# Seven half-width products for the up projection of every second pair, and running sums copied from bank to bank by ScalarE

## The chip, the cores and the metric

The kernel runs on one core of one Trainium2 chip. The metric is the device time of one execution in microseconds (us). Weights and activations are split into a high and a low part, so that three matmuls (high by high, low by high, high by low) stand for one exact fp32 product; each full-size product therefore costs three matmuls for every 128 rows of the contraction.

## The reference

One layer of a macaron block on 512 tokens of width 1024: a SwiGLU network, a token mixer, a second SwiGLU network, each added to the stream, and a last norm. Only the two SwiGLU networks are touched here:

```python
D_MODEL = 1024
SEQ = 512
D_FF = 256 * ((8 * D_MODEL // 3 + 255) // 256)      # 2816
...
def swiglu(x, w_gate, w_up, w_down):
    return (jax.nn.silu(x @ w_gate) * (x @ w_up)) @ w_down
...
        x = x + 0.5 * swiglu(rmsnorm(x, ffn1_norm[layer]),
                             ffn1_w_gate[layer], ffn1_w_up[layer], ffn1_w_down[layer])
        x = x + token_mixer(...)
        x = x + 0.5 * swiglu(rmsnorm(x, ffn2_norm[layer]),
                             ffn2_w_gate[layer], ffn2_w_up[layer], ffn2_w_down[layer])
```

## The kernel before

Everything is kept transposed: features on the 128 partitions, the 512 tokens along the free axis. The hidden width of 2816 is 22 tiles of 128 columns, numbered j; the model width is 8 tiles, numbered k. The function `ffn` runs twice, as network "a" and network "b"; a letter a or b at the end of a tile's name tells which.

The first n1 tiles of a network (6 in a, 4 in b) are computed singly. The rest are taken two at a time by `pair(j)`: j = 6, 8, ..., 20 in a (8 pairs), j = 4, 6, ..., 20 in b (9 pairs). For a pair the gate projection is a 2-by-2 block product (two column tiles, the even and the odd k tiles, the left and the right 256 tokens), and it is done by Winograd's form of Strassen's method: seven products of half width instead of eight. Each of the seven is a call of `product`: four k tiles times three matmuls, 12 matmuls of 128x256. The sums of token blocks that it needs are made once per network (`normed_t`). The sums of weight blocks are made anew for every pair on VectorE (lines 266 to 273): `s1`, `s2`, the difference written into `r1`, and a second value of `s2`. Then each of seven weight blocks of 128x512 is split: ScalarE writes the high part (line 261), VectorE subtracts and writes the low part (line 262).

In PSUM the gate products of a pair use four banks of the tag "mm", half of each: pa (named pw), pb (px), pc (py), pd (pz). ScalarE copies the first product from pa into half of the tile `sq` (line 296), VectorE adds pb to that (298), and the further sums are made by VectorE from pd, pc and that tile (301, 302, 306, 309). The banks pa, pd and pc are used for two products each; where the second product adds into a sum that VectorE must read first, TensorE waits for that read (line 301 reads pd before the product with `a22` goes on in it; line 302 reads pc before the product with `w4`).

The up projection of a pair is done plainly by `up`, once for each of the two tiles: 8 k tiles times three matmuls of 128x512, 24 matmuls, weights loaded as one tile of 128x1024 and split by one wide cast (line 91) and one wide subtraction (line 92). VectorE then multiplies gate and up (line 313), and `activated` splits the result (lines 188 and 189) for the down projection.

What sets the order: TensorE runs in the order of the program text. ScalarE, VectorE and the DMA queue run in an order that the compiler's scheduler fixes ahead of time, from the dependences and the free buffers; on the chip each engine follows its own list strictly. The buffers matter: the tags "raw", "wh" and "wl" (incoming weights, high parts, low parts) have three buffers of 128x1024 each, "ob" (for `s1`, `s2`) two, "ptb" (for the gate tiles `g0`, `g1`) two, and PSUM has four banks "mm", two "s" and two "t". A gate product takes four wh and four wl buffers in turn, a single up tile one of each. In the first pair of each network the two up projections stand ahead of the gate products, so that there the gate products of two pairs follow one another directly.

Of the kernel before, what the change touches and what calls it, by code (L numbers as in the profile page):

```python
# [25 lines left out]
JF = FF // P  # L26
# [12 lines left out]

EARLY = (5, 3)  # L40
PAIRED = (6, 4)
HS = S // 2
F32_MAX = 3.4028234e38
PSUM = bass.MemoryType.PSUM
# [5 lines left out]
def tile_macaron(ctx: ExitStack, tc, xs, xT, wf, wgu1, wst1, wd1, wqk, wv, wo, wgu2, wst2, wd2,  # L50
                 lams, relb, onehot, addc, out):
    nc = tc.nc
    V, A, G, T = nc.vector, nc.scalar, nc.gpsimd, nc.tensor
# [13 lines left out]
    def mm_bank(nm):  # L67
        return pp.tile([P, S], F32, tag="mm", name=nm, bufs=4)
# [5 lines left out]
    sq = cp.tile([P, S], F32, tag="sq", name="sq")  # L74
# [8 lines left out]
    def load_w(src, nm, n=1024):  # L83
        raw = wp.tile([P, 1024], F32, tag="raw", name=f"raw_{nm}")
        nc.sync.dma_start(raw[:, :n], src)
        h = wp.tile([P, 1024], F32R, tag="wh", name=f"wh_{nm}")
        l = wp.tile([P, 1024], F32R, tag="wl", name=f"wl_{nm}")
        return raw, h, l

    def split_w(raw, h, l, a, b):  # L90
        A.copy(h[:, a:b], raw[:, a:b])  # L91
        V.tensor_tensor(l[:, a:b], raw[:, a:b], h[:, a:b].bitcast(F32), op=ALU.subtract)  # L92

    def get_w(src, nm, n=1024):
        raw, h, l = load_w(src, nm, n)
        split_w(raw, h, l, 0, n)
        return h, l

    def mm3(po, wh, wl, mh, ml, first, last, on=False):
        T.matmul(po, wh, mh, start=first, stop=False, skip_group_check=on)  # L100
        T.matmul(po, wh, ml, start=False, stop=False, skip_group_check=on)  # L101
        T.matmul(po, wl, mh, start=False, stop=last, skip_group_check=on)  # L102
# [72 lines left out]
    def ffn(wgu, wst, wd, n0, n1, norm, early, res, nm, hooks, first=None, last_halves=None):  # L175
# [39 lines left out]
        def t_places():  # L215
            tp.tile([P, 8], F32, tag="odd", name=f"odd{nm}", bufs=1)
            rows = [tp.tile([P, 5 * HS], F32R, tag=f"pr{p % 2}", name=f"tt{nm}{p}")
                    for p in range(4)]
            more = tp.tile([P, 12 * HS], F32R, tag="tx", name=f"tx{nm}", bufs=1)
            tl.extend(t[:, :4 * HS] for t in rows)  # L220
            th.extend(more[:, 4 * p * HS:4 * (p + 1) * HS] for p in range(3))
            th.append([t[:, 4 * HS:] for t in rows])

        def normed_t(p):
# [22 lines left out]
            c = slice(half * HS, (half + 1) * HS)  # L247
            return xh[k][:, c], xl[k][:, c]

        def pair(j):  # L250
            src = [wst[j + i - n1] for i in range(2)]
            ups = [up(j + i, src[i][1]) for i in range(2)] if j == n1 else []
            (r0, h0, l0), (r1, h1, l1) = [load_w(src[i][0], f"sg{nm}{j + i}") for i in range(2)]
            u0, u1 = slice(0, 512), slice(512, 1024)
            h2, l2, h3, l3 = [wp.tile([P, 1024], F32R, tag=t, name=f"{t}_{i}{nm}{j}")
                              for i in (2, 3) for t in ("wh", "wl")]
            s1 = tp.tile([P, S], F32, tag="ob", name=f"s1{nm}{j}")
            s2 = tp.tile([P, S], F32, tag="ob", name=f"s2{nm}{j}")

            def split(t, h, l):  # L260
                A.copy(h, t)
                V.tensor_tensor(l, t, h.bitcast(F32), op=ALU.subtract)
                return h, l

            a11 = split(r0[:, u0], h0[:, u0], l0[:, u0])
            V.tensor_tensor(s1[:], r1[:, u0], r1[:, u1], op=ALU.add)
            V.tensor_tensor(s2[:], s1[:], r0[:, u0], op=ALU.subtract)
            w2 = split(s2[:], h0[:, u1], l0[:, u1])
            w1 = split(s1[:], h1[:, u0], l1[:, u0])
            V.tensor_tensor(r1[:, u0], r0[:, u0], r1[:, u0], op=ALU.subtract)  # L270
# [6 lines left out]
            pa, pb, pc, pd = [mm_bank(f"p{c}{nm}{j}")[:, :HS] for c in "wxyz"]  # L277

            def product(po, w, mv, first, last):
                for p in range(4):  # L280
                    o = slice(p * P, (p + 1) * P)
                    mm3(po, w[0][:, o], w[1][:, o], *mv(p), first and p == 0, last and p == 3, not first)

            def b(i, half):
                return lambda p: block(2 * p + i, half)

            def t(i):
                c = slice(i * HS, (i + 1) * HS)
                return lambda p: (th[p][i] if p == 3 else th[p][:, c], tl[p][:, c])

            g0 = tp.tile([P, S], F32, tag="ptb", name=f"g0{nm}{j}")
            g1 = tp.tile([P, S], F32, tag="ptb", name=f"g1{nm}{j}")
            w = sq[:, :HS] if (j // 2) % 2 else sq[:, HS:]
            left, right = slice(0, HS), slice(HS, S)
            product(pa, a11, b(0, 0), True, True)
            A.copy(w, pa)
# [4 lines left out]
            V.tensor_tensor(g1[:, right], pd, w, op=ALU.add)  # L301
# [7 lines left out]
            V.tensor_tensor(g0[:, right], pc, w, op=ALU.add)  # L309
            A.activation(g0[:, right], g0[:, right], AF.Silu)  # L310
            for i, g in enumerate((g0, g1)):
                pu = ups[i] if ups else up(j + i, src[i][1])
                V.tensor_tensor(g[:], pu[:], g[:], op=ALU.mult)
                activated(j + i, g)

        def up(j, src):
            wh, wl = get_w(src, f"su{nm}{j}")
            pu = pp.tile([P, S], F32, tag="t", name=f"pu{nm}{j}", bufs=2)
            for k in range(KD):
                o = slice(k * P, (k + 1) * P)  # L320
# [18 lines left out]
        for j in range(j0, n1):  # L339
            mv = (eh, el) if j < n0 else (xh, xl)  # L340
            if j == 2 and first is not None:
                pg, pu = [pp.tile([P, S], F32, tag="t", name=f"p{c}{nm}2", bufs=2) for c in "gu"]
            else:
                pg = mm_bank(f"pg{nm}{j}")
                pu = mm_bank(f"pu{nm}{j}")
            for hf in range(2):
                wh, wl = get_w(wgu[j, hf], f"gu{nm}{j}_{hf}")
                for kk in range(4):
                    k = hf * 4 + kk
                    for c, pt in ((0, pg), (1, pu)):  # L350
                        o = kk * 256 + c * P
# [12 lines left out]
        for m in range(KD):  # L364
# [36 lines left out]
    with tc.manual_schedule(engines={mybir.EngineType.DVE, mybir.EngineType.Activation}):  # L401
        for t in range(4):
# [3 lines left out]
            for kk in range(2):  # L406
                k = 2 * t + kk
# [627 lines left out]
```

## Time and profile before

| | us |
|---|---|
| median of three runs | 976.99 |
| lowest and highest | 976.98 and 978.43 |
| the profiled execution | 977.07 |
| its span in the profile | 974.8 |
| TensorE busy | 961.4 (99%) |
| VectorE busy | 577.6 (59%) |
| ScalarE busy | 426.0 (44%) |

The profiled execution lies 0.08 us from the median, and 2.27 us of it lie outside the span. In the rows of the timeline the first number is the start in us from the span's start, the second the duration; then come the engine, the line, the operation and what it writes from what. PE is TensorE's matmul, DVE is VectorE, ACT is ScalarE. A matmul's recorded duration is longer than the distance to the next one, since matmuls overlap; the distance between starts is what counts.

### The profile page before, as it was taken

To read this page: it belongs to the slowest core of one execution; us is meant where nothing else is said; L and a number is where in the kernel's file an instruction comes from. 1 tells how busy PE (TensorE), PEld (TensorE's weight loads), DVE (VectorE), ACT (ScalarE), POOL (GpSimd) and SP (SyncE) were. 2 spreads that over 40 slices of the span, in tenths; PEclk is the share of its full clock that TensorE was granted. 3 is DMA by queue.
4 is the path that set the end of the run, shared out by engine and by line. 5 is a ranking of instruction groups with operands and counts; after the bars stand their busy time and mean duration, and the time that the engine had idled before them with its cause. 6 is when DMAs were issued, how large, how long until landed. Compare 5 with 4: busy or idle time off the path is not lost.

```text
span 974.8 us, 13809 instructions
## 1 busy us (share of the span) xinstructions
PE 961.4 (99%) x5394; PEld 839.6 (86%) x5394; DVE 577.6 (59%) x1108; ACT 426.0 (44%) x787; POOL 32.4 (3%) x34
## 2 busy tenths in 40 slices
PE   9999999999999999999999999999999999999996
PEld 7789998888788888988989888889988899888886
DVE  7698767765232336668764546797677566422223
ACT  6455444434232335566756554454444344322230
POOL 0000000000010110000000003000000000000110
PEclk9999999999999999999999999999999999999998
DMA  7232423224333351444342204232332233433312
GB/s 253 66 114 67 130 91 118 95 87 130 98 97 84 96 160 62 130 119 120 88 112 85 76 32 130 65 108 73 118 114 87 87 101 117 119 98 84 96 58 87
DMA packets 32720, 98.71 MB, mean 101 GB/s; under 512 B 3776, under 2 KB 6080, under 8 KB 32656
## 3 DMA queue, kind: packets, MB, share of 16 engines
q1 hardware_dynamic: 32480, 97.55, 32.8%
q8 instruction: 42, 0.69, 0.3%
q0 software_dynamic: 176, 0.30, 0.1%
q14 instruction: 22, 0.18, 0.1%
HBM read 92.55 MB, written 2.14 MB: 97 GB/s over the span
## 4 chain that ended last, share of the span: by engine, by line
PE 94%; DVE 3%; ACT 1%; DMA 1%; issue 1%; DVEq 0%; POOL 0%; ACTq 0%; POOLq 0%
PE pda L100 4%; PE pub L100 4%; PE pub L101 4%; PE pda L102 4%; PE pda L101 4%; PE pub L102 4%; PE pua L100 4%; PE pua L101 4%; PE pua L102 4%; PE pdb L101 4%; PE pdb L100 4%; PE pdb L102 4%; PE po L704 2%; PE pwo L100 1%; PE pwo L101 1%; PE pwo L102 1%
## 5 line engine op out<-in xcount | busy, mean ns | idle before, releaser
L100 PE MATMUL pda<-aha,wh_da 128*128 128x512 f32 x176 | 68.6, 390 | 0.0
L102 PE MATMUL pda<-aha,wl_da 128*128 128x512 f32 x176 | 68.5, 389 | 0.0
L101 PE MATMUL pda<-ala,wh_da 128*128 128x512 f32 x176 | 68.5, 389 | 0.0
L92 DVE TENSOR_TENSOR wl_db<-raw_db,wh_db 128x1024 fp32r<-128x1024 f32 (+1 forms) x24 | 27.3, 1136 | 62.2 <-ACT wh_db L91 62.1
L92 DVE TENSOR_TENSOR wl_da<-raw_da,wh_da 128x1024 fp32r<-128x1024 f32 (+1 forms) x24 | 27.2, 1135 | 58.7 <-ACT wh_da L91 58.6
L91 ACT CAST wh_db<-raw_db 128x1024 fp32r<-128x1024 f32 (+1 forms) x24 | 23.6, 981 | 86.2 <-PE pdb L101 78.7
L91 ACT CAST wh_da<-raw_da 128x1024 fp32r<-128x1024 f32 (+1 forms) x24 | 23.5, 981 | 84.2 <-PE pda L101 55.5
L101 PE MATMUL pdb<-alb,wh_db 128*128 128x512 f32 x154 | 59.9, 389 | 0.0
L102 PE MATMUL pdb<-ahb,wl_db 128*128 128x512 f32 x154 | 59.9, 389 | 0.0
L100 PE MATMUL pdb<-ahb,wh_db 128*128 128x512 f32 x154 | 59.9, 389 | 0.0
L100 PE MATMUL pub<-xh,wh_sub 128*128 128x512 f32 x144 | 56.1, 390 | 0.0
L101 PE MATMUL pub<-xl,wh_sub 128*128 128x512 f32 x144 | 56.1, 390 | 0.0
L102 PE MATMUL pub<-xh,wl_sub 128*128 128x512 f32 x144 | 56.0, 389 | 0.0
L670 DVE CUSTOM_DVE_ANT_0 pr<-sc,strip 128x128 f32<-128x128 f32 (+3 forms) x64 | 30.8, 488 | 34.0 <-PE sc L668 33.6
L127 POOL TENSOR_TENSOR sq<-sq,sqt 128x512 f32<-128x512 f32 x20 | 28.7, 1435 | 661.8 <-ACT sqt L126 661.8
L100 PE MATMUL pua<-xh,wh_sua 128*128 128x512 f32 x128 | 49.9, 390 | 0.0
L101 PE MATMUL pua<-xl,wh_sua 128*128 128x512 f32 x128 | 49.9, 390 | 0.0
L102 PE MATMUL pua<-xh,wl_sua 128*128 128x512 f32 x128 | 49.8, 389 | 0.0
L673 ACT ACTIVATE pr<-pr,mx 128x128 f32<-128x128 f32 (+3 forms) x64 | 36.0, 563 | 30.8 <-DVE mx L670 29.7
L100 PEld LDWEIGHTS pda<-aha,wh_da 128*128 128x128 f32 x176 | 33.0, 188 | 7.3 <-ACT wh_da L91 0.5
L101 PEld LDWEIGHTS pda<-ala,wh_da 128*128 128x128 f32 x176 | 33.0, 188 | 6.9
L102 PEld LDWEIGHTS pda<-aha,wl_da 128*128 128x128 f32 x176 | 33.0, 188 | 6.9
(470 smaller groups left out, 2889.7 us busy)
## 6 DMA issues: line engine op xcount, KB each, us to landing
raw_sub<-wst_dram SPq DMA_DIRECT2D x18, 512.0 KB, 3.6
raw_sgb<-wst_dram SPq DMA_DIRECT2D x18, 512.0 KB, 3.7
raw_sua<-wst_dram SPq DMA_DIRECT2D x16, 512.0 KB, 3.5
raw_sga<-wst_dram SPq DMA_DIRECT2D x16, 512.0 KB, 3.8
raw_da<-wd_dram SPq DMA_DIRECT2D x16, 512.0 KB, 3.6
raw_qk<-wqk_dram SPq DMA_DIRECT2D x16, 512.0 KB, 3.6
raw_db<-wd_dram SPq DMA_DIRECT2D x16, 512.0 KB, 3.5
raw_gua<-wgu_dram SPq DMA_DIRECT2D x8, 512.0 KB, 3.6
```

Source lines behind the costliest of these rows:

```text
L91: A.copy(h[:, a:b], raw[:, a:b])
L92: V.tensor_tensor(l[:, a:b], raw[:, a:b], h[:, a:b].bitcast(F32), op=ALU.subtract)
L100: T.matmul(po, wh, mh, start=first, stop=False, skip_group_check=on)
L101: T.matmul(po, wh, ml, start=False, stop=False, skip_group_check=on)
L102: T.matmul(po, wl, mh, start=False, stop=last, skip_group_check=on)
L127: G.tensor_tensor(sq[:], sq[:], t[:], op=ALU.add)
L670: V.tensor_tensor_reduce(out=pi, in0=ps[:, :w], in1=st["b"][m][:, w - 1::-1], op0=ALU.add, op1=ALU.min, scale=1.0, scalar=3.0e38, accum_ou ...
L673: A.activation(pi, pi, AF.Exp, scale=-1.0, bias=st["mx"][:, m, i:i + 1], accum_out=st["ls"][:, m, i:i + 1])
L704: T.matmul(st["po3"][:, i, d0:d0 + dn], st["ptb", m, i][:, k * P:(k + 1) * P], vt[u // 4, k][:, fo + d0:fo + d0 + dn], start=k == 0, stop= ...
```

## The change

Two things are changed in `pair`. First, the seven products become a generator, `seven`, in another order and with other sums: the first product is made in pa, ScalarE copies it into pb, the product with `w2` goes on adding in pb, ScalarE copies that sum into pc, and the product with `w1` goes on adding in pc. The product with `w3`, alone in pd, is copied by ScalarE into SBUF (`p7`; for the gate that is half of the tile that held the norm's factors). VectorE's five additions become two. Second, for the pairs in `UP_PAIRS` (j = 8, 12, 16, 20, in both networks, so 8 of the 17 pairs) the up projection is made by the same generator, in the PSUM banks s, t, t, s, with `sq` for `p7`; the other pairs keep two plain up products. The up weights are laid out by the host with even k tiles first, as the gate's were; `up` reads them accordingly.

```diff
+UP_PAIRS = range(8, JF, 4)
...
-            w2 = split(s2[:], h0[:, u1], l0[:, u1])
-            w1 = split(s1[:], h1[:, u0], l1[:, u0])
-            V.tensor_tensor(r1[:, u0], r0[:, u0], r1[:, u0], op=ALU.subtract)
-            w3 = split(r1[:, u0], h1[:, u1], l1[:, u1])
-            a12 = split(r0[:, u1], h2[:, u0], l2[:, u0])
+            V.tensor_tensor(r1[:, u0], r0[:, u0], r1[:, u0], op=ALU.subtract)
+            w3 = split(r1[:, u0], h0[:, u1], l0[:, u1])
+            V.tensor_tensor(s2[:], s1[:], r0[:, u0], op=ALU.subtract)
+            w2 = split(s2[:], h1[:, u0], l1[:, u0])
+            a12 = split(r0[:, u1], h1[:, u1], l1[:, u1])
+            w1 = split(s1[:], h2[:, u0], l2[:, u0])
+            a22 = split(r1[:, u1], h2[:, u1], l2[:, u1])
             V.tensor_tensor(s2[:], r0[:, u1], s2[:], op=ALU.subtract)
-            a22 = split(r1[:, u1], h2[:, u1], l2[:, u1])
             w4 = split(s2[:], h3[:, u0], l3[:, u0])
...
+            pa, pb, pc, pd = banks
+            product(pa, a11, b(0, 0), True)
+            A.copy(pb, pa)
+            product(pd, w3, t(1), True)
+            A.copy(p7, pd)
+            product(pb, w2, t(3))
+            A.copy(pc, pb)
+            product(pa, a12, b(1, 0))
+            yield pa
+            product(pc, w1, t(0))
+            yield pc
+            product(pb, a22, t(2))
+            yield pb
+            product(pc, w4, b(1, 1))
+            yield pc
...
-            product(pa, a11, b(0, 0), True, True)
-            A.copy(w, pa)
-            product(pb, w2, t(3), True, True)
-            V.tensor_tensor(w, pb, w, op=ALU.add)
-            product(pc, w1, t(0), True, True)
-            product(pd, w3, t(1), True, True)
-            V.tensor_tensor(g1[:, right], pd, w, op=ALU.add)
-            V.tensor_tensor(g1[:, right], pc, g1[:, right], op=ALU.add)
-            product(pa, a12, b(1, 0), False, True)
-            A.activation(g0[:, left], pa, AF.Silu)
-            product(pd, a22, t(2), False, True)
-            V.tensor_tensor(g1[:, left], pd, w, op=ALU.add)
+            p7 = res["bc"][:, left]
+            run = seven(j, 0, half_banks(("mm", "mm", "mm", "mm"), j), p7)
+            A.activation(g0[:, left], next(run), AF.Silu)
+            V.tensor_tensor(g1[:, right], next(run), p7, op=ALU.add)
+            V.tensor_tensor(g1[:, left], next(run), p7, op=ALU.add)
             A.activation(g1[:], g1[:], AF.Silu)
-            product(pc, w4, b(1, 1), False, True)
-            V.tensor_tensor(g0[:, right], pc, w, op=ALU.add)
-            A.activation(g0[:, right], g0[:, right], AF.Silu)
+            A.activation(g0[:, right], next(run), AF.Silu)
+            if j in UP_PAIRS:
+                p7 = sq[:, left]
+                run = seven(j, 1, half_banks(("s", "t", "t", "s"), f"u{j}"), p7)
+                V.tensor_tensor(g0[:, left], next(run), g0[:, left], op=ALU.mult)
+                V.tensor_tensor(sq[:, right], next(run), p7, op=ALU.add)
+                V.tensor_tensor(sq[:, left], next(run), p7, op=ALU.add)
+                V.tensor_tensor(g1[:], sq[:], g1[:], op=ALU.mult)
+                V.tensor_tensor(g0[:, right], next(run), g0[:, right], op=ALU.mult)
+                activated(j + 1, g1)
+                activated(j, g0)
+                return
```

More of the change, by code (lines that the diff above doesn't have):

```diff
@@ L248, in block, with seven @@
             return xh[k][:, c], xl[k][:, c]
[L250 to L253, printed above, removed]
+        def seven(j, c, banks, p7):
+            (r0, h0, l0), (r1, h1, l1) = [load_w(wst[j + i - n1][c], f"s{c}{nm}{j + i}")
+                                          for i in range(2)]
             u0, u1 = slice(0, 512), slice(512, 1024)
-            h2, l2, h3, l3 = [wp.tile([P, 1024], F32R, tag=t, name=f"{t}_{i}{nm}{j}")
+            h2, l2, h3, l3 = [wp.tile([P, 1024], F32R, tag=t, name=f"{t}_{i}{c}{nm}{j}")
                               for i in (2, 3) for t in ("wh", "wl")]
-            s1 = tp.tile([P, S], F32, tag="ob", name=f"s1{nm}{j}")
-            s2 = tp.tile([P, S], F32, tag="ob", name=f"s2{nm}{j}")
+            s1 = tp.tile([P, S], F32, tag="ob", name=f"s1{c}{nm}{j}")
+            s2 = tp.tile([P, S], F32, tag="ob", name=f"s2{c}{nm}{j}")
             def split(t, h, l):
@@ L291, in pair, with half_banks @@
+            product(pc, w4, b(1, 1))
+            yield pc
+        def half_banks(tags, j):
+            return [pp.tile([P, S], F32, tag=t, name=f"p{c}{nm}{j}", bufs=4 if t == "mm" else 2)
+                    [:, :HS] for t, c in zip(tags, "wxyz")]
+        def pair(j):
+            ups = [up(j + i) for i in range(2)] if j == n1 else []
             g0 = tp.tile([P, S], F32, tag="ptb", name=f"g0{nm}{j}")
             g1 = tp.tile([P, S], F32, tag="ptb", name=f"g1{nm}{j}")
-            w = sq[:, :HS] if (j // 2) % 2 else sq[:, HS:]
@@ L311, in pair, with up @@
             for i, g in enumerate((g0, g1)):
-                pu = ups[i] if ups else up(j + i, src[i][1])
+                pu = ups[i] if ups else up(j + i)
                 V.tensor_tensor(g[:], pu[:], g[:], op=ALU.mult)
                 activated(j + i, g)
-        def up(j, src):
-            wh, wl = get_w(src, f"su{nm}{j}")
+        def up(j):
+            wh, wl = get_w(wst[j - n1][1], f"su{nm}{j}")
             pu = pp.tile([P, S], F32, tag="t", name=f"pu{nm}{j}", bufs=2)
             for k in range(KD):
-                o = slice(k * P, (k + 1) * P)
+                o = k // 2 * P + k % 2 * 4 * P
+                o = slice(o, o + P)
@@ L989, in block_tiles @@
     def block_tiles(g, u, n):
[L991 to L993 removed]
+        t = np.stack([col_tiles(w)[n:].reshape(JF - n, P, KD, P) for w in (g, u)], axis=1)
+        t = np.concatenate([t[:, :, :, 0::2], t[:, :, :, 1::2]], axis=3)
+        return np.ascontiguousarray(t).reshape(JF - n, 2, P, KD * P)
     wi = a(w_in[0])
```

8 lines of the change are left out of this document (2 added, 6 removed).

## The prediction

> **What bounds the kernel now.** I read first the page's engine totals and its chain that ended last.
>
> ```profile
> PE 961.4 (99%) x5394; PEld 839.6 (86%) x5394; DVE 577.6 (59%) x1108; ACT 426.0 (44%) x787; POOL 32.4 (3%) x34
> PE 94%; DVE 3%; ACT 1%; DMA 1%; issue 1%; DVEq 0%; POOL 0%; ACTq 0%; POOLq 0%
> ```
>
> TensorE is busy all the time and the chain is TensorE's own work. Then the list of TensorE's waits: within the pairs it holds two short ones, both for the read of pd on line 301.
>
> ```profile
> PE pzb L100 <- DVE g1b L301: 0.3, 1, 0.3
> PE pza L100 <- DVE g1a L301: 0.2, 1, 0.2
> ```
>
> So time falls only if TensorE gets less to do, and each new wait of TensorE is paid in full. Third, one steady pair of network a in two stretches, gate products and plain up products (columns: stretch, length, then busy us and instructions of PE, weight loads, DVE, ACT):
>
> ```profile
> 136.52:146.49 9.97, 9.97 (x85) 9.96 (x84) 6.38 (x11) 5.41 (x9) 0.00 (x0) 1.00 0.39 123
> 146.49:157.40 10.91, 10.91 (x51) 9.02 (x49) 7.66 (x12) 3.48 (x8) 0.00 (x0) 1.00 0.26 83
> sum 20.88, PE 20.88 PEld 18.98 DVE 14.04 ACT 8.89 POOL 0.00; mean PE 10.44 PEld 9.49 DVE 7.02 ACT 4.45 POOL 0.00
> ```
>
> TensorE has no gap in 20.88 us; VectorE has 6.84 us idle, ScalarE 12.0.
>
> **TensorE's work.** The ends of those stretches are starts of matmuls on the timeline:
>
> ```profile
> 136.52 0.28 PE L100 MATMUL pwa<-xh,wh_sga 128*128 128x256 f32 x1
> 137.84 0.28 PE L102 MATMUL pwa<-xh,wl_sga 128*128 128x256 f32 x1
> 137.96 0.28 PE L100 MATMUL pxa<-txa,wh_sga 128*128 128x256 f32 x1
> 138.16 0.37 ACT L296 COPY sq<-pwa 128x256 f32<-128x256 f32 x1
> 139.38 0.28 PE L100 MATMUL pya<-txa,wh_sga 128*128 128x256 f32 x1
> 142.20 0.28 PE L100 MATMUL pwa<-xh,wh_2a 128*128 128x256 f32 x1
> 146.49 0.40 PE L100 MATMUL pua<-xh,wh_sua 128*128 128x512 f32 x1
> 157.40 0.28 PE L100 MATMUL pwa<-xh,wh_sga 128*128 128x256 f32 x1
> ```
>
> Seven products, 84 matmuls of half width, take 146.49 - 136.52 = 9.97 us (0.119 each); the 48 wide up matmuls take 157.40 - 146.49 = 10.91 us (0.227 each). Replacing the second by the first saves 0.94 us; in 8 pairs 7.5 us. The gate products stay 84 matmuls, in another order.
>
> The Trainium skill, "TensorE: Matmul & The Clock Gate", section "Back-to-back issue gap", gives N/2.4 + 2.5 ns for a warm matmul alone, 109 and 216 ns here; by it the saving would be 1.2 us a pair, 9.5 in all. The distances above are about 10 ns longer, so the rows decide.
>
> **A wait that goes.** The two waits on line 301, on the timeline:
>
> ```profile
> 90.74 0.68 DVE L270 TENSOR_TENSOR raw_sga<-raw_sga,raw_sga 128x512 f32<-128x512 f32 x1
> 91.34 0.42 DVE L301 TENSOR_TENSOR g1a<-pza,sq 128x256 f32<-128x256 f32 x1
> 91.35 0.28 PE L102 MATMUL pwa<-xh,wl_2a 128*128 128x256 f32 x1
> 91.81 0.39 PE L100 MATMUL pza<-txa,wh_2a 128*128 128x256 f32 x1 [0.19 <-DVE g1a L301]
> 92.04 0.28 PE L101 MATMUL pza<-tta,wh_2a 128*128 128x256 f32 x1
> 671.60 0.28 PE L102 MATMUL pwb<-xh,wl_2b 128*128 128x256 f32 x1
> 672.18 0.39 PE L100 MATMUL pzb<-txb,wh_2b 128*128 128x256 f32 x1 [0.31 <-DVE g1b L301]
> 672.40 0.28 PE L101 MATMUL pzb<-ttb,wh_2b 128*128 128x256 f32 x1
> ```
>
> The read sat behind a 0.60 us step of the next pair's weights. TensorE started 0.05 after the read ended, 0.34 late, and the next matmul came 0.23 instead of 0.12 later (the weight load had not run ahead): 0.45 us, and by the same count 0.56 in b. After the change a22 no longer follows a read of its bank by VectorE: -1.0 us. The same rows price a late read elsewhere: to cost nothing it must end 0.16 ahead of the matmul.
>
> **Copies between banks.** The product with w2 now waits for the copy of pa into pb, the one with w1 for the copy of pb into pc; all of TensorE's further work queues behind each. Between a product and its continuation stands one other product, 139.38 - 137.96 = 1.42 us. The copy above started 0.20 after the last product's slot ended and took 0.37; adding 0.16 leaves 0.69 us. A copy that writes PSUM is in no row; from below it cannot cost TensorE less than nothing, since TensorE loses no work by it; from above, each copy of the 50 (25 calls of seven, two each) pays if ScalarE is held by over 0.69. I take nothing: in a call no ScalarE step queued near it is longer than a 0.62 cast, and ScalarE's share is worked out next. If the cover went, each 0.1 us late would cost 5 us in all.
>
> **VectorE and ScalarE in a pair of the new kind.** Durations by shape, in that pair:
>
> ```profile
> L92 DVE TENSOR_TENSOR wl_sua<-raw_sua,wh_sua 128x1024 fp32r<-128x1024 f32 x2 | 2.5, 1225 | 0.7 <-ACT wh_sua L91 0.5
> L91 ACT CAST wh_sua<-raw_sua 128x1024 fp32r<-128x1024 f32 x2 | 2.1, 1050 | 3.1 <-PE pza L101 3.1
> L261 ACT CAST wh_2a<-raw_sga 128x512 fp32r<-128x512 f32 x3 | 1.8, 621 | 7.4 <-PE pua L101 7.4
> L262 DVE TENSOR_TENSOR wl_sga<-raw_sga,wh_sga 128x512 fp32r<-128x512 f32 x2 | 1.4, 682 | 0.0
> L301 DVE TENSOR_TENSOR g1a<-pza,sq 128x256 f32<-128x256 f32 x1 | 0.4, 426 | 1.5 <-PE pza L102 1.5
> ```
>
> and the starts, since an operation starts before the last one's recorded end:
>
> ```profile
> 142.33 1.05 ACT L91 CAST wh_sua<-raw_sua 128x1024 fp32r<-128x1024 f32 x1 [2.20 <-PE pza L101]
> 142.40 0.43 DVE L301 TENSOR_TENSOR g1a<-pza,sq 128x256 f32<-128x256 f32 x1 [1.55 <-PE pza L102]
> 145.14 1.05 ACT L91 CAST wh_sua<-raw_sua 128x1024 fp32r<-128x1024 f32 x1 [0.92 <-PE pza L101]
> 146.22 1.22 DVE L92 TENSOR_TENSOR wl_sua<-raw_sua,wh_sua 128x1024 fp32r<-128x1024 f32 x1 [0.54 <-ACT wh_sua L91]
> 147.36 0.42 DVE L309 TENSOR_TENSOR g0a<-pya,sq 128x256 f32<-128x256 f32 x1
> 147.70 0.68 DVE L262 TENSOR_TENSOR wl_sga<-raw_sga,wh_sga 128x512 fp32r<-128x512 f32 x1
> 148.30 0.69 DVE L266 TENSOR_TENSOR s1a<-raw_sga 128x512 f32<-128x512 f32 x1
> 149.02 0.69 DVE L267 TENSOR_TENSOR s2a<-s1a,raw_sga 128x512 f32<-128x512 f32 x1
> ```
>
> On VectorE a wide subtraction occupies 1.14, a half 0.60 (0.72 where it needs the one before it), a quarter 0.34. A new pair drops two wide ones (-2.28) and three quarter additions of the gate (-1.02), gains seven low parts (+4.2) and four sums (+2.6), and replaces two half multiplications by four quarter operations and one half (+0.76): 14.04 + 4.3 = 18.3 of the pair's new length, 2 x 9.97 = 19.94. That is 92%, with 1.6 us to spare. ScalarE drops two wide casts (-2.1), gains seven halves (+4.3) and five copies (+1.85): 8.89 + 4.05 = 12.9, 65%.
>
> At 92% a read will often find a step ahead of it. Only one kind of read holds TensorE: the product with w4 continues in pc after VectorE has read pc. The product with a22 covers 1.42; the read may start 0.20 after w1's product (142.20 to 142.40), takes 0.42, and 0.16 must be left: a margin of 0.64, one half step and no more. Lower bound 0; upper bound two half steps and a bit, 1.0. I take 0.45, the first measured wait, for the up half of each new pair, since it is the nearest row: there too seven products followed seven products, and one row of queued steps was too many. 8 x 0.45 = +3.6.
>
> In the seven plain pairs whose gate comes ahead of the ups (10, 14, 18 in a; 6, 10, 14, 18 in b) the freed weight buffer now lets the wide up cast in just before that read: cast 0.13 after the fourth product (142.20 to 142.33), 1.05, then 0.03, the subtraction occupies 1.14: the read starts at 2.35, ends 2.77, and should end by 2.84 - 0.16 = 2.68. 0.09 late, 7 x 0.09 = +0.6; nothing if the read is queued first, 0.5 each if the cast slips further.
>
> **Free edits.** The new split order only follows the products; the first weights of an up half wait for the gate's fourth product, three products (4.2 us) ahead of their use, against two casts and two subtractions of 0.6. The number of DMA loads and their bytes stay; a load for the next gate can start once the up half's blocks are split, some 5 us before its use ends the cover (512 KB land in under 4 us):
>
> ```profile
> raw_sga<-wst_dram SPq DMA_DIRECT2D x16, 512.0 KB, 3.8
> ```
>
> If that cover went, VectorE's first sum would be late and the next gate with it. It is thinnest where three calls of seven meet (pairs 6 and 8 of a); that is in the range. The moved read order in `up` and the PSUM banks cost nothing: banks s are idle in the networks' pairs and each t bank is read a whole gate earlier.
>
> **Sum**, against the profiled execution of 977.07 (0.08 above the median): -7.5 - 1.0 + 3.6 + 0.6 = -4.3, 972.8 us.
>
> **Rivals.**
> 1. No waits: the reads are queued first. 977.07 - 8.5 = 968.5. For it: 1.6 us spare; against it: both transitions with seven after seven waited. Chance 0.18.
> 2. Eaten up: each up half waits 0.9. 968.5 + 7.2 + 0.6 = 976.3, no change. 0.12.
> 3. Slower, VectorE becomes the bound: it needs 18.3 us and in each new pair keeps idling for casts and reads. With 3.0 us idle (today 6.84) the pair takes 21.3 instead of 19.94: 8 x 1.4 = 11 on top of 969.1, 980. It turns slower beyond 2.6 us idle. For it: the 1.5 us idle ahead of line 301 above; against it: that idleness exists because nothing else was queued. 0.12.
> 4. ScalarE's list puts the cast for w4 (it waits for a buffer until w3's product is done) ahead of the copy into pb. Then the copy starts 0.13 + 0.62 after w3's product, takes 0.37, and with the 0.16 TensorE loses 1.3 us in each of 25 calls, 32 in all: about 1000. Against it: line 296 stands right after its product today. 0.03.
> 5. Half-width matmuls are paced by their weight loads, not their columns:
>
> ```profile
> L102 PEld LDWEIGHTS pwb<-xh,wl_2b 128*128 128x128 f32 x36 | 6.9, 191 | 0.0
> ```
>
> 84 x 0.191 = 16.0 against the 10.91 that go: 8 x 5.1 = 41 us lost, 1017. The starts 0.12 apart refute it: 0.01. The same section of the Trainium skill's page gives sustained figures of 81 ns at N=128 and 131 at N=512, by which half-width products would also be the slower way; the 0.227 of this trace contradicts it.
>
> That a copied sum were not added to would change no time.
>
> **Numbers.** Forecast 0.54, rivals 0.18, 0.12, 0.12, 0.03, 0.01. A difference of 0.2%, 1.95 us, is about what can be told from no change here. Faster by more: 0.54 + 0.18 + 0.02 of the second rival = 0.74; within: 0.10; slower: 0.16. The range from 968.4 (rival 1) to 977.6 (rival 2 with the 0.5 of some plain pairs) leaves out rivals 3 to 5, 0.16.
>
> **What would show it.** Up halves of 9.97 us plus a wait; in TensorE's waits a row for pc (py of the up half) behind VectorE's read of it, about 0.3 each; none on the copies; none on the bank of a22; VectorE above 85% busy in new pairs. Wrong would be: a wait on a copy, an up half over 10.9, or waits for low parts of weights.

## The result, and the profile after

The kernel after the change takes 973.43 us (median of 5 runs, 972.51 to 973.61) where the one before takes 976.99 (976.19 to 978.43, 5 runs on the same chip): ratio 0.9959, 95% interval 0.9944 to 0.9973, a gain of 0.4%. The profiled execution of the kernel after takes 972.58 us with a span of 970.3, 4.5 less than the 977.07 and 974.8 of before. The prediction, 972.8, lay 0.6 below the median.

From the page of the kernel after, the engine totals and the chain that ended last:

```profile
PE 957.1 (99%) x5682; PEld 848.8 (87%) x5682; DVE 599.6 (62%) x1153; ACT 454.9 (47%) x885; POOL 32.4 (3%) x34
PE 90%; DVE 5%; ACT 2%; DMA 1%; issue 1%; DVEq 0%; POOL 0%; SPq 0%; ACTq 0%; POOLq 0%
```

TensorE executes 288 matmuls more (8 x 36) and is busy 4.3 us less. VectorE's and ScalarE's shares of the chain have grown from 4% together to 7%: TensorE now waits for them more often. The busy time of each engine in three stretches (columns as in the prediction): the gate of pair 12 of network a, its up half, and the gate of pair 14.

```profile
136.19:146.15 9.96, 9.96 (x85) 9.96 (x84) 7.88 (x14) 5.96 (x13) 0.00 (x0) 1.00 0.21 72
146.15:156.42 10.27, 10.23 (x87) 10.02 (x85) 8.46 (x16) 5.82 (x13) 0.00 (x0) 1.00 0.30 105
156.42:166.48 10.06, 10.06 (x87) 10.03 (x85) 7.22 (x13) 6.16 (x12) 0.00 (x0) 1.00 0.39 127
```

The up half takes 10.27 instead of 10.91, 0.30 more than its 84 matmuls need; the next gate, in front of plain ups, is 0.10 longer than a clean one. VectorE is busy 16.34 of the new pair's 20.23 us, 81%. The list of the weight loads' waits (engine, tile, line, what they waited for, us in total, times, longest) names both kinds of wait that lie in the pairs:

```profile
PEld pybu L102 <- DVE sq L329: 0.6, 3, 0.2
PEld pxa L102 <- ACT pxa L295: 0.5, 2, 0.3
PEld pyau L102 <- DVE sq L329: 0.5, 2, 0.3
PEld pxb L102 <- ACT pxb L295: 0.2, 1, 0.2
```

L329 is the up half's read of pc, L295 the copy of pa into pb. TensorE's own list has no row for the pairs, since the recorded end of a matmul reaches over waits this short; the starts of the products on the timeline show them. For each kernel the table below sums, over both networks, the time from the first gate product of the pairs to the first matmul of the down projection, and the part by which products took longer than a clean one (1.416 us for 12 matmuls, 1.4375 for the two products in pa). It is worked out from every product's start; "up halves" counts the up projections done by seven products.

| kernel | up halves | stretch of pairs, us | of it waits, us | median, us |
|---|---|---|---|---|
| before | 0 | 334.06 | 1.2 | 977 to 978 |
| after | 8 | 329.12 | 3.9 | 973.43 |
| 1 new gates, old ups | 0 | 334.85 | 2.0 | 978.42 |
| 2 seven products in all ups but the first | 15 | 340.70 | 22.1 | 984.88 |
| 3 old gates, new up halves | 8 | 329.07 | 3.9 | 972.88 |
| 4 sum s1 on GpSimd | 8 | 334.93 | 9.7 | 978.85 |
| 5 w4 goes on in a fourth bank | 8 | 326.46 | 1.2 | 970.82 |
| 6 reads first | 8 | 340.85 | 15.6 | 985.41 |
| 7 reads and copies first | 8 | 335.86 | 10.6 | 979.59 |
| 8 as 7, all ups | 15 | 338.72 | 20.2 | 981.72 |
| 9 fourth bank, all ups | 15 | 336.58 | 18.0 | 981.45 |
| 10 fourth bank, casts later | 8 | 326.07 | 0.9 | 969.39 |
| 11 fourth bank, all ups, casts later | 15 | 325.09 | 6.5 | 967.71 |
| 12 as 9, low parts later | 15 | 340.48 | 21.9 | 983.97 |

Take the waits away from the stretch, and what is left depends on the number of up halves alone: 332.8 to 332.9 with none, 325.2 with eight, 318.6 with fifteen. So an up half saves 0.95 us of TensorE's work wherever it is put, and everything else in this table is waiting. The change as it stands: 334.06 - 329.12 = 4.94 less in the pairs. The span is only 4.5 shorter because of the stretch from the start of the last two matmuls to the end, which has the same work in every kernel: it takes 7.06 in the profile before and 7.58 after. Both lengths also occur among the other profiles (7.05 to 7.94 in all), so the 0.5 is not of the change.

### The profile page after: what moved, and what is told of

The parts are those of the page before. It is cut to its first block, busy times and chain, and to the rows that moved or that the text cites. A ratio compares the mean times of both kernels' runs of the same rounds, so it can differ in the third digit from the quotient of the medians.

```text
span 970.3 us, 14564 instructions
## 1 busy us (share of the span) xinstructions
PE 957.1 (99%) x5682; PEld 848.8 (87%) x5682; DVE 599.6 (62%) x1153; ACT 454.9 (47%) x885; POOL 32.4 (3%) x34
## 4 chain that ended last, share of the span: by engine, by line
PE 90%; DVE 5%; ACT 2%; DMA 1%; issue 1%; DVEq 0%; POOL 0%; SPq 0%; ACTq 0%; POOLq 0%
PE pda L102 4%; PE pda L104 4%; PE pda L103 4%; PE pdb L102 4%; PE pdb L103 4%; PE pdb L104 4%; PE pub L103 3%; PE pub L104 3%; PE pub L102 3%; PE pua L102 3%; PE pua L103 3%; PE pua L104 3%; PE po L730 2%; PE pwo L102 1%; PE pwo L103 1%; PE pwo L104 1%
## 5 line engine op out<-in xcount | busy, mean ns | idle before, releaser
L730 PEld LDWEIGHTS po<-v,ptb 128*128 128x128 f32 x240 | 32.7, 191 | 4.9 <-ACT ptb L720 2.3
L588 PE MATMUL pv<-wh_v,xh 128*128 128x256 f32 x128 | 36.2, 283 | 0.0
L590 PE MATMUL pv<-wl_v,xh 128*128 128x256 f32 x128 | 36.2, 283 | 0.0
L589 PE MATMUL pv<-wh_v,xl 128*128 128x256 f32 x128 | 36.2, 283 | 0.0
L104 PEld LDWEIGHTS pdb<-ahb,wl_db 128*128 128x128 f32 x154 | 28.9, 188 | 6.0
L102 PEld LDWEIGHTS pdb<-ahb,wh_db 128*128 128x128 f32 x154 | 28.9, 188 | 6.0
```

What stands on the lines that cost most here:

```text
L588: T.matmul(po, xh[k][:, xs], wh[:, o:o + 256], start=k == 0, stop=False)
L589: T.matmul(po, xl[k][:, xs], wh[:, o:o + 256], start=False, stop=False)
L590: T.matmul(po, xh[k][:, xs], wl[:, o:o + 256], start=False, stop=k == KD - 1)
L730: T.matmul(st["po3"][:, i, d0:d0 + dn], st["ptb", m, i][:, k * P:(k + 1) * P], vt[u // 4, k][:, fo + d0:fo + d0 + dn], start=k == 0, stop= ...
```

## The experiments

Each ratio is to the kernel before, run beside it on the same chip (medians 977.53 to 978.43). Since the same kernel differs by that much from one chip and session to the next, small differences between experiments are read from the ratios and the waits, not from the medians. Line numbers are those of the kernel that was run; "..." marks lines left out. "Theory of the list" in the expectations is explained in experiment 4.

**1. The new gates alone.**

```
-UP_PAIRS = range(8, JF, 4)
+UP_PAIRS = ()
```

> UP_PAIRS empty: all 17 pairs keep plain up products, the gate products are the new ones. Theory A (TensorE pays for single steps queued ahead of a read or a copy): the two waits of before on line 301 go (-1.0), each of some 15 plain gates waits 0.1 before w4 (+1.5) and the two gates that follow a gate directly wait some 0.25 on the copy into pb (+0.5): 977.99 - about 1.0, so 977 to 978, no gain. Theory B (waits come only when VectorE's load nears 100%): plain pairs have VectorE idle, no wait at all, 976.0. 84 x 17 gate matmuls and 48 x 17 up matmuls either way.

978.42 us, ratio 1.0011 (1.0002 to 1.0019). The two waits of a22 behind line 301 are gone, and in their place stand 0.10 before w4 in nearly every gate and 0.27 or 0.28 on a copy once in each network. By itself the new gate gains nothing, and loses about 0.8 us in the pairs: theory A's case, a little above its 978. Theory B, no wait at all while VectorE has time to spare, doesn't hold.

**2. Seven products in the ups of every pair but each network's first.**

```
-UP_PAIRS = range(8, JF, 4)
+UP_PAIRS = range(6, JF, 2)
...
-            if j in UP_PAIRS:
+            if j in UP_PAIRS and not ups:
```

> UP_PAIRS is every pair but the first of each network: 7 in a, 8 in b, 15 instead of 8. Theory A (a fixed wait of about 0.3 in each up half and 0.1 to 0.4 in each gate that follows one): 15 x 0.94 + 1.0 = 15.1 saved, 15 x 0.3 + 15 x 0.3 given back: about 971. Theory B (VectorE needs 18.3 of 19.94 us in each such pair, and here no plain pair lies between in which it catches up): waits grow, pairs take over 20.9 us, 977 or more.

984.88 us, ratio 1.0071 (1.0058 to 1.0083): seven more up halves take 6.7 us of work away, and the waits grow by 18. The time is the one that theory B named, but VectorE isn't full (17.59 of 21.64 us, 81%, in the pair that begins at 158.21). Its timeline, the transfer that SP (SyncE) issues and the matmul that waits, in that pair's gate:

```profile
162.62 0.69 DVE L266 TENSOR_TENSOR wl_20a<-raw_s0a,wh_20a 128x512 fp32r<-128x512 f32 x1
163.38 0.33 SPq L87 DMA_DIRECT2D raw_s1a<-wst_dram  x1
167.15 0.69 DVE L270 TENSOR_TENSOR s11a<-raw_s1a 128x512 f32<-128x512 f32 x1 [1.20 <-DMA raw_s1a<-wst_dram]
167.76 0.42 DVE L321 TENSOR_TENSOR g1a<-pya,rbc_n 128x256 f32<-128x256 f32 x1
168.32 0.36 PE L102 MATMUL pya<-xh,wh_30a 128*128 128x256 f32 x1 [1.04 <-DVE g1a L321]
```

VectorE stands idle for 1.20 us with the read that TensorE needs next in its list. The sum s1 of the next call is ahead of that read and waits for its second raw tile. There are three raw buffers, and two calls want four, so that transfer could start only when the call before gave one back. It was issued 0.07 after the low part of a22 ended (162.62 + 0.69), the last step that reads that call's second raw tile; the low part stands in VectorE's list behind that call's other steps.

**3. The old gates with the new up halves.**

```
-            p7 = res["bc"][:, left]
-            run = seven(j, 0, half_banks(("mm", "mm", "mm", "mm"), j), p7)
...
+            w = res["bc"][:, left]
+            product(pa, a11, b(0, 0), True, True)
+            A.copy(w, pa)
...
+            V.tensor_tensor(g0[:, right], pc, w, op=ALU.add)
+            A.activation(g0[:, right], g0[:, right], AF.Silu)
             if j in UP_PAIRS:
```

> The gate products as before (old order, sums on VectorE, the reads of pd and pc both ahead of further products), the up projection of the 8 pairs by seven as in the change. Theory A: 7.5 saved as in the change, but three more quarter steps on VectorE in each pair, and two reads for TensorE to wait for in each gate: at least 1.0 us more waits than the change in the two networks, 973.5 to 976. Rival C (the new gate order is of no account): the same as the change, 972.5 to 973.5.

972.88 us, ratio 0.9953 (0.994 to 0.9965): not to be told from the kernel after, rival C's case, where 973.5 to 976 had been expected by theory A. (The old gate's running sum lies in the tile of the norm's factors here, since `sq` serves the up half.) The waits sum to the same 3.9 us, but they are fewer and larger; from the list of the weight loads' waits:

```profile
PEld pybu L102 <- DVE sq L377: 1.4, 1, 1.4
PEld pzb L102 <- DVE g1b L363: 1.2, 2, 0.8
```

L363 is the old gate's read of pd (line 301 before the change). So the rewritten gate is of no account for the time: it trades one set of waits for another. The gain is that of the up halves.

**4. The first sum on GpSimd**, in all 25 calls, which takes 0.7 us of work from VectorE in each.

```
-            V.tensor_tensor(s1[:], r1[:, u0], r1[:, u1], op=ALU.add)
+            G.tensor_tensor(s1[:], r1[:, u0], r1[:, u1], op=ALU.add)
```

> As the change, but the first sum of weight blocks (s1) is made by GpSimd in all 25 calls of seven. VectorE has 0.6 to 0.7 us less in each call. Theory B (VectorE's load makes the waits): the 1.8 us in up halves and the 0.8 before w4 in gates fall below half, 971.5. Theory A: which step stands ahead of the read decides; VectorE's list changes but waits of the same size stay, 972.5 to 973.5. Third: GpSimd's 1.4 us a sum instead of 0.7 delays the weights of the next call and adds waits where one seven follows another, slower than the change by 0.5 to 1.

978.85 us, ratio 1.0011 (1.0002 to 1.002): VectorE has less to do and TensorE waits 5.8 us longer. Theory B is refuted; the third text has the direction, but named only 0.5 to 1. The steps behind one another in an up half:

```profile
153.53 1.29 POOL L270 TENSOR_TENSOR s10a<-raw_s0a 128x512 f32<-128x512 f32 x1 [11.62 <-DMA raw_s0a<-wst_dram]
154.85 0.69 DVE L271 TENSOR_TENSOR raw_s0a<-raw_s0a,raw_s0a 128x512 f32<-128x512 f32 x1 [1.88 <-POOL s10a L270]
157.59 0.42 DVE L329 TENSOR_TENSOR sq<-pyau,sq 128x256 f32<-128x256 f32 x1
158.07 0.39 PE L102 MATMUL pyau<-xh,wh_31a 128*128 128x256 f32 x1 [0.73 <-DVE sq L329]
```

GpSimd takes 1.29 for this sum instead of 0.69; VectorE's difference r1 = r0 - r1 (line 271) overwrites what the sum reads, so it must wait, and the read of pc is further back in the same list. It isn't VectorE's load that makes the read late but what stands ahead of it, and when that can run. In the kernel after, the same chain in the same pair:

```profile
146.71 0.68 DVE L278 TENSOR_TENSOR s21a<-raw_s1a,s21a 128x512 f32<-128x512 f32 x1
147.46 0.33 SPq L87 DMA_DIRECT2D raw_s0a<-wst_dram  x1
150.95 0.69 DVE L270 TENSOR_TENSOR s10a<-raw_s0a 128x512 f32<-128x512 f32 x1 [0.47 <-DMA raw_s0a<-wst_dram]
152.29 0.68 DVE L273 TENSOR_TENSOR s20a<-s10a,raw_s0a 128x512 f32<-128x512 f32 x1
153.22 1.28 DVE L266 TENSOR_TENSOR wl_s0a<-raw_s0a,wh_s0a 128x512 fp32r<-128x512 f32 x2
154.43 0.42 DVE L329 TENSOR_TENSOR sq<-pyau,sq 128x256 f32<-128x256 f32 x1
154.89 0.19 PEld L102 LDWEIGHTS pyau<-xh,wh_31a 128*128 128x128 f32 x1 [0.25 <-DVE sq L329]
```

The load starts at 147.46, when the up half's last sum is done with the buffer, and lands 3.5 us later; from 150.95 to 155.0 VectorE works without a gap on the next call's sums and low parts and then on the read. The product with w1 ended at 153.28; the read starts 1.15 after that. This I call the theory of the list; its rival is that VectorE simply has too little time.

**5. The read out of TensorE's way.** ScalarE copies pc into pd once w1 is done, and w4 goes on in pd.

```
             product(pc, w1, t(0))
             yield pc
+            A.copy(pd, pc)
             product(pb, a22, t(2))
             yield pb
-            product(pc, w4, b(1, 1))
-            yield pc
+            product(pd, w4, b(1, 1))
+            yield pd
```

> ScalarE also copies pc into pd once w1 is done, and the product with w4 goes on in pd; VectorE still reads pc, but nobody waits for that read any more. Theory of the list (TensorE's waits before w4 are for VectorE's read, which stands in VectorE's fixed list behind the next call's sums): the 1.8 us before w4 of the up halves and the 0.5 us of the plain gates go, the 0.9 us on copies at the start of a gate stay; about 971.1. Rival (ScalarE is as late as VectorE, the copy queues behind casts that wait for weight buffers): the waits only change their name; 973 to 976. Rival (VectorE is short of time): its late steps show up as waits for low parts; 973 or more.

970.82 us, ratio 0.9931 (0.9919 to 0.9944). All waits before w4 are gone; of the 1.2 us that are left, 0.8 are on the copy of pa into pb in three gates, the rest is spread over products that each lose less than 0.06. The same place on the timeline:

```profile
153.24 0.36 ACT L303 COPY pzau<-pyau 128x256 f32<-128x256 f32 x1 [0.41 <-PE pyau L104]
154.11 0.42 DVE L330 TENSOR_TENSOR sq<-pyau,sq 128x256 f32<-128x256 f32 x1
```

VectorE reads as late as it did, and nobody waits for it; ScalarE copies 0.87 earlier. The theory of the list gave 971.1.

**6. The reads first.** Everything that VectorE does for the next call is queued behind the last call's read of pc; the plain ups likewise. The work and TensorE's list are the same as in the kernel after. (`tc.issue_after(x)` puts the steps of its block that run on x's engine behind x in that engine's list.)

```
+            queue = ExitStack()
+            if read:
+                queue.enter_context(tc.issue_after(read[-1].ins))
             a11 = split(r0[:, u0], h0[:, u0], l0[:, u0])
...
             w4 = split(s2[:], h3[:, u0], l3[:, u0])
+            queue.close()
...
-            V.tensor_tensor(g1[:, right], next(run), p7, op=ALU.add)
+            read.append(V.tensor_tensor(g1[:, right], next(run), p7, op=ALU.add))
...
```

> In VectorE's list all sums and low parts of the next call of seven, and of the plain ups, stand behind the last call's read of pc; TensorE's list, the loads and the amount of work stay. Theory of the list: the waits before w4 fall from 2.3 us to near 0, the copies' 0.9 stay; about 971.1. Rival (VectorE is short of time): TensorE then waits at the next call for low parts of w3 or w2, 0.3 us or more in each of eight places; 973.5 or more.

985.41 us, ratio 1.0076 (1.0062 to 1.009), 12 more than the kernel after, where 971.1 had been expected: this is the rival's case, at several times its price. The main row of the weight loads' waits in network a:

```profile
PEld pxa L102 <- ACT wh_s0a L266: 3.5, 3, 1.2
```

How it comes about, on the timeline (L334 is the read of pc, L277 the sum s2, which is w2):

```profile
151.90 0.33 SPq L87 DMA_DIRECT2D raw_s0a<-wst_dram  x1
155.87 0.42 DVE L334 TENSOR_TENSOR sq<-pyau,sq 128x256 f32<-128x256 f32 x1 [0.99 <-PE pyau L104]
161.09 0.68 DVE L277 TENSOR_TENSOR s20a<-s10a,raw_s0a 128x512 f32<-128x512 f32 x1
161.84 0.62 ACT L266 CAST wh_s0a<-s20a 128x512 fp32r<-128x512 f32 x1
```

The read no longer waits, but w2's sum, done at 152.3 to 153.0 in the kernel after, now comes at 161.09, and its cast ends at 162.46, 1.1 us after TensorE wanted w2. From the read at 155.87 to TensorE's need for w2 at 161.38 lie 5.5 us, in which VectorE works without a gap and isn't done. Nor could it have begun much sooner: the up half's own steps were moved back in the same way, so that the load for s1 is issued 3.6 us after the up half's start (148.30) instead of 1.3, and lands at 155.58. On the average of a pair VectorE has time free (a fifth in the kernel after); in this stretch it has none, and part of what the planner puts ahead of the read has to stand there.

**7. As 6, and the two casts of a pair's results behind the next gate's first copy** in ScalarE's list.

```
-            A.copy(pb, pa)
+            copied = A.copy(pb, pa)
...
             A.copy(p7, pd)
+            with tc.issue_after(copied.ins):
+                while later:
+                    activated(*later.pop(0))
...
-                activated(j + 1, g1)
-                activated(j, g0)
+                later.extend(((j + 1, g1), (j, g0)))
...
```

The next pair's gate tiles `g0` and `g1` are taken after its first products here, and in 8 and 10 to 12, so that the moved steps can still read the last pair's.

> As the run before, and the two casts of a pair's results (the activated values) stand behind the next gate's copy of pa into pb in ScalarE's list. Theory of the list: the 0.9 us of waits for that copy go as well; 970.2. Rival: the casts of the next gate's weights move to the same place, the copies stay late; 971.

979.59 us, ratio 1.0022 (1.0013 to 1.0032). 5 us of waits less than in 6, since the results' low parts no longer stand between VectorE and w2 either; 970.2 or, by the rival, 971 was expected, so neither text holds.

**8. As 7, all ups but each network's first** (the edit of 2).

> The run before with seven products in the ups of every pair but the first of each network: seven pairs more. Theory of the list: each saves 0.94 us, 6.6 in all, and the 1.0 us before w4 of each gate is gone; 964 to 967. Rival (the late load of the next call's second weights is the limit, whatever the order): the sums move behind the read, and w3 and w2 of the next gate are late instead; 975 to 985.

981.72 us, ratio 1.0046 (1.0033 to 1.0058), within the rival's 975 to 985 and outside the theory's 964 to 967. The largest row of its weight loads' waits is one for a low part of the next call:

```profile
PEld pxb L104 <- DVE wl_s0b L267: 3.8, 8, 0.5
```

**9. The fourth bank (5), all ups but the first (2), the planner's order.**

> The fourth bank for w4 (as in the run where only that was done) and seven products in the ups of every pair but the first of each network, in the planner's own order. With the order of steps left alone and VectorE's reads out of TensorE's way, the 1.0 us before w4 in each gate behind an up half should be gone. Theory of the list: 970.8 - 7 x 0.94 = 964.2, plus 0.3 for the copy at each of 7 more meetings of up half and gate, 966.3. Rival (ScalarE's third copy is held up by the casts of late weights, or the low parts of the next call come late): 0.5 to 1.0 in each of 15 meetings; 973 to 980.

981.45 us, ratio 1.0042 (1.0029 to 1.0056), the rival's case and a little beyond its 980: no wait before w4, but 0.7 to 1.0 at the start of 13 up halves. One of them:

```profile
160.10 0.68 DVE L191 TENSOR_TENSOR ala<-g1a,aha 128x512 fp32r<-128x512 f32 x1
160.71 0.69 DVE L191 TENSOR_TENSOR ala<-g0a,aha 128x512 fp32r<-128x512 f32 x1
161.91 0.68 DVE L266 TENSOR_TENSOR wl_20a<-raw_s0a,wh_20a 128x512 fp32r<-128x512 f32 x1
162.67 0.33 SPq L87 DMA_DIRECT2D raw_s1a<-wst_dram  x1
166.32 0.69 DVE L270 TENSOR_TENSOR s11a<-raw_s1a 128x512 f32<-128x512 f32 x1 [1.09 <-DMA raw_s1a<-wst_dram]
169.53 0.19 PEld L104 LDWEIGHTS pzau<-txa,wl_s1a 128*128 128x128 f32 x1 [0.39 <-DVE wl_s1a L266]
```

The gate began at 157.25. The low part of a22, which frees the buffer as in experiment 2, comes 4.66 us later, behind the low parts of the last pair's results (L191); the load starts 0.08 after its end, at 162.67, s1 at 166.32, and the low part of w3 is late in the up half that began at 167.51.

**10. The fourth bank and the casts of 7, eight up halves, without the reads first.**

> The fourth bank for w4 with UP_PAIRS as in the kernel after, and in ScalarE's list the two casts of a pair's results behind the next gate's copy of pa into pb. Theory of the list: the wait for that copy (about 0.9 us in all in the kernel after, 0.2 to 0.3 at each of three meetings of up half and gate) goes; 970.0 to 970.4. Rival: what is moved holds the low parts of w3 or w2; 971 or more.

969.39 us, ratio 0.9916 (0.9903 to 0.993): 0.85 us of waits left, and none where an up half meets a gate. What is left on that copy lies in the two gates that follow a gate directly, 0.24 and 0.22, where the casts are those of a pair with plain ups and were not moved. The wait on the copy that is taken away here, as the kernel after has it:

```profile
116.34 0.62 ACT L190 CAST aha<-g1a 128x512 fp32r<-128x512 f32 x1
116.86 0.62 ACT L190 CAST aha<-g0a 128x512 fp32r<-128x512 f32 x1
117.38 0.36 ACT L295 COPY pxa<-pwa 128x256 f32<-128x256 f32 x1
117.80 0.19 PEld L102 LDWEIGHTS pxa<-txa,wh_s0a 128*128 128x128 f32 x1 [0.30 <-ACT pxa L295]
```

The first product of that gate ended at 116.1; the copy could have started at 116.34, 1.0 us earlier, but for two casts of the pair before.

**11. Both: the fourth bank, all ups but the first, the casts behind the copy.**

> Both of the two runs above together. Theory of the list: 964.2 to 965. Rival: the casts of the results now hold up the casts of the next gate's weights at 15 meetings, 0.3 us or more each; 969 or more.

967.71 us, ratio 0.9896 (0.9883 to 0.991), the fastest version: below the kernel after and the kernel before. (Its interval meets that of 10, so that the two can't be told apart with certainty.) The same place as in 9 (the L267 row is the low part of a22 here, L271 is s1):

```profile
157.27 0.36 ACT L296 COPY pxa<-pwa 128x256 f32<-128x256 f32 x1 [0.27 <-PE pwa L104]
157.54 0.62 ACT L191 CAST aha<-g1a 128x512 fp32r<-128x512 f32 x1
158.79 0.68 DVE L267 TENSOR_TENSOR wl_20a<-raw_s0a,wh_20a 128x512 fp32r<-128x512 f32 x1
159.50 0.33 SPq L87 DMA_DIRECT2D raw_s1a<-wst_dram  x1
163.23 0.69 DVE L271 TENSOR_TENSOR s11a<-raw_s1a 128x512 f32<-128x512 f32 x1 [0.42 <-DMA raw_s1a<-wst_dram]
```

The gate began at 155.63; the low part of a22 comes 3.16 us later, not 4.66, and s1 7.6 us later, not 9.1. The up half behind it loses 0.1 instead of 1.0. The work is the same as in 9; 11.5 us of waits are gone with two casts and two low parts moved. 6.5 us stay, so that the time lies between the two texts. This is also the plainest answer to the rival that VectorE simply has too little time: in the pair shown here it is busy for 17.47 of 20.09 us (87%), in the same pair of 9 for 17.47 of 21.25 (82%), and yet the waits in the pairs are 6.5 us here and 18.0 there.

**12. As 9, with only the results' low parts moved**, behind the next gate's last sum on VectorE; ScalarE's casts stay where the planner puts them.

```
-            V.tensor_tensor(s2[:], r0[:, u1], s2[:], op=ALU.subtract)
+            freed = V.tensor_tensor(s2[:], r0[:, u1], s2[:], op=ALU.subtract)
+            with tc.issue_after(freed.ins):
+                while later:
+                    later.pop(0)()
```

> The run with the fourth bank and seven products in all ups but the first, at 981.45, with one thing moved: in VectorE's list the two low parts of a pair's results stand behind the next gate's last sum (s2 from the second half of r0), which is the last step that holds r0's buffer. ScalarE's order stays, the casts of the results ahead of the copy. Theory of the late load (those two low parts delay the last sum by 1.2 us, so the next call's second raw load starts 1.2 us later, its sums are late and TensorE waits for the low part of w3 and then for the copy): the 0.7 to 1.0 us at the start of each up half fall to 0.2 or less, 13 x 0.7 = 9 less; the 0.2 to 0.3 on the copy in each gate stay; about 970 to 973. Rival (ScalarE's late copies are the cause, as the run with the casts behind the copy would also allow): hardly a change, 978 to 982.

983.97 us, ratio 1.0062 (1.0048 to 1.0075): neither text. (The text takes the last sum for the step that holds the buffer; in run 9 it was the step ahead of it, the low part of a22, but the two moved low parts stood ahead of both.) At the start of the up halves the waits fell as expected (0.2 to 0.7 in six, under 0.1 in the others; the load is issued 3.7 us after the gate's start instead of 5.4). But the waits on the first copy in the gates, 0.2 to 0.5 in run 9, grew to as much as 1.2, and in nine gates new ones of 0.5 to 1.7 us appeared, on the copy of pc into pd (L311):

```profile
PEld pzb L102 <- ACT pzb L311: 5.3, 5, 1.7
```

One of these on the timeline (L270 is a cast of the next call's weights):

```profile
161.38 0.33 SPq L87 DMA_DIRECT2D raw_s1a<-wst_dram  x1
165.97 0.69 DVE L275 TENSOR_TENSOR s11a<-raw_s1a 128x512 f32<-128x512 f32 x1 [2.26 <-DMA raw_s1a<-wst_dram]
167.42 0.62 ACT L270 CAST wh_s1a<-raw_s1a 128x512 fp32r<-128x512 f32 x1 [2.26 <-DVE raw_s1a L276]
167.95 0.37 ACT L311 COPY pza<-pya 128x256 f32<-128x256 f32 x1
```

With VectorE's order changed the planner put the cast for w3 ahead of the copy on ScalarE. That cast waits for r1, r1 for the load, and the copy stands behind it although the product with w1 was done at 165.56. It is the chain of experiment 2 again, on the other engine. The load is issued early here, but lands 4.6 us after its issue, where 9 and 11 have 3.6 and 3.7 at this place; why isn't shown. How much of the gain of 11 is the earlier load and how much the earlier copy, this run doesn't separate.

## Why the prediction was right, and where it wasn't

- **TensorE's work, -7.5**: the table, without the waits, gives 332.9 - 325.2 = 7.6, rounded from 332.86 and 325.22. The distances between matmul starts were the right price.
- **The wait of a22, -1.0**: no wait on that bank is left in the kernel after.
- **The up halves' read, +3.6**: right in mechanism, half in size. 0.10 to 0.34 each, 1.8 in all, where 0.45 each was taken. In the last pair of each network, with no call behind it, only 0.10. What I had seen as "one row of queued steps too many" is a row whose start is set by a load.
- **The plain gates' read, +0.6**: 0.10 in five of the seven, 0.27 and 0.07 in the other two, 0.87 in all, and 0.2 more in the gate of pair 8. The cover was as thin as worked out.
- **Copies, "I take nothing"**: this step failed, and the prediction itself had named a wait on a copy as a sign of being wrong. They cost 0.9: 0.27 and 0.26 where a gate follows a gate, 0.36 where the gate of pair 10 follows the up half of pair 8. The margin of 0.69 was right (counted as in the prediction, ScalarE was held by 0.97 in the gate of pair 8 of network a and by 1.06 in that of pair 10, 0.28 and 0.37 over the margin); the reason, that no step near the copy is longer than a 0.62 cast, overlooked two such casts in a row, those of the pair before, at the place where two calls meet.
- **"Thinnest where three calls of seven meet"**: it is, and the waits there (pairs 6, 8 and the gate of 10) are 1.3 of the 3.8 us in waits of 0.05 or more. The named reason, the load cover, holds for the smaller part of them: the reads in the gate and the up half of pair 8, 0.4 together, stand behind a sum that waited for its load. The other 0.9 are the copies above, behind the casts, and the read in the gate of pair 10, behind a plain up's low part. I had put the price in the range and not in the sum.
- **VectorE at 92%**: per pair the extra work was near the 4.3 us estimated (599.6 - 577.6 = 22.0 us in all, with 9 x 1.02 saved in the other gates: 3.9 for each new pair), but part of it is done in the stretches beside the pair, and the 20.23 us have 16.34. That is 81%, so the sign "above 85% busy in new pairs" was not met. Rival 3, VectorE as the bound, is not what happened; experiment 6 shows the place where it would be.
- **The sum**: 4.3 less was forecast; the profiled executions show 4.5 less, the medians 3.6. Waits of 4.2 were forecast, 3.8 were found (1.8 + 1.1 + 0.9), with a term that was taken as nothing standing for one that was twice too large. That the total is nearer than its parts is luck.

The Trainium skill's "TensorE: Matmul & The Clock Gate", "Back-to-back issue gap", would have made the up halves save 9.5 us by its rule for a matmul alone, columns over the clock plus a fixed gap. The table's 7.6 says that here the distances between starts decide.

## What to carry to other kernels

In this kernel, where TensorE is always busy, taking matmuls away paid at the distance of their starts, and all the rest was a question of which step stood ahead of TensorE's next need in the other engines' fixed lists. How busy VectorE was on average (81% of a new pair in the kernel after, 87% in run 11) did not tell which. Look for the first step in the list that waits for a transfer, and for the step that lets that transfer start. Moving two low parts and two casts took 11.5 us of waits away here (run 11 against 9), and moving the reads that seemed to be late added 11.7 (run 6 against the kernel after). A copy that takes a bank out of an engine's way (run 5) can be cheaper than making the engine read in time (run 6).

## What the hardware showed that was not expected

- A copy from one bank to another takes ScalarE 0.36 us for 128x256 in the kernel after, about the same as one into SBUF (0.36 to 0.37 there). It was in no row before.
- The same 128x512 sum takes GpSimd 1.29 us in the gates of experiment 4 (1.6 to 1.7 in most up halves) and VectorE 0.69 in the kernel after.
- A bank that comes free late costs twice: in the two waits on line 301 in the prediction's rows the matmul starts about 0.05 us after the release, and the next one follows 0.22 to 0.23 later instead of 0.12. The shortest waits in the kernel after likewise show as 0.10 in a product's length.
